# Twelve instead of eight of the 22 up tiles of a gated MLP as transposed seven-product blocks, and both token sublayers in a new order

## The chip, the cores and the metric

The kernel runs on one core of a Trainium2 chip. The metric is the device time of one execution in microseconds (us). TensorE is called PE here, VectorE DVE, ScalarE ACT, GpSimd POOL and SyncE SP; PEld is the loading of weights into PE, which runs beside its matmuls.

## The reference, cut to what matters

Two layers (`DEPTH` = 2) on 512 tokens of width 1024, everything in f32. Each layer has a token sublayer and a channel sublayer:

```python
proj = x @ w_in[i]                       # q, k, v of two kinds of heads, and three gates
ya = neighbourhood_attention(...)        # 8 heads of 64
yb = bidirectional_retention(...)        # 4 heads, chunks of 128 tokens
merged = sigmoid(gate_a) * (ya @ w_branch_a[i]) + sigmoid(gate_b) * (yb @ w_branch_b[i])
x = layer_norm(ALPHA * x + merged @ w_out[i], ...)
h = x @ w_up[i]                          # 1024 -> 2 * 2816, then a convolution of width 3 over tokens
ffn = (gelu(a) * b) @ w_down[i]          # a, b: the two halves of the convolved h
ple = sigmoid(x @ w_ple_gate[i]) * (p[i] @ w_ple_proj[i])
x = layer_norm(ALPHA * x + ffn + ple, ...)
```

## The kernel before, in words

**Arithmetic.** Each f32 matrix is carried as two fp32r matrices, hi and lo (`split`, L177: ACT casts hi, DVE subtracts hi from the source and gives lo). A product is three matmuls, hi·hi, hi·lo and lo·hi (`mm3`, L432; their records have L434, L435 and L436). Where `_Ordered` (L95) holds an engine to the order of the program, everything that is issued through it shows as L109.

**Seven products.** Most of the large matrix products run as 2x2 block products in seven steps instead of eight: a, c, t1, t2, d, t3 and t4, of which t1, t2, d and t3 take sums of blocks of the activations and sums of blocks of the weights. The results go through two PSUM pairs, u and v, and a third one for c.

**Weights.** All weights lie in DRAM in chunks of 128x1024 (512 KB). `Stream` (L304) holds the list of all chunks in the order of their use. It loads a chunk by a DMA that SP issues (`fetch`, L348), adds a second block to it, where a sum is wanted, by an accumulating DMA that POOL issues (`add`, L335; L342), and splits it (`prep`, L373). A few items are "sent": ACT makes hi and then minus hi in the place of lo, and a DMA of POOL adds the weights to that (L392 to L394), so that DVE has nothing to do with them. The `HELD`, `EARLY` and `DEEP` tables say where a raw chunk lies and how far ahead of its use it is loaded and split.

**Token sublayer.** The combined projection runs first as blocks of seven products for v and gates (`VG`), with the heads' q and k, the attention and the retention woven in by the list `FILL`. `bb` (L1153) is the product with `w_branch_b`, `ba` (L1141) that with `w_branch_a`; `turn` (L1131) transposes the merged rows; `proj_ln` (L511) is the output projection with the layer norm, and its transposes are in `done1` (L1292). `plain_x` (L1117) brings the residual in rows: in layer 0 it only loads it, in layer 1 it loads the normalised values and multiplies by the gain and adds the bias on DVE (L1126, L1127), four times each over 128x1024. It is called at product number `XN_AT` of `bb`.

**Channel sublayer.** 22 up tiles are handled in segments of 6, 8 and 8 (`SEGS` counts pairs); each segment's down product (`D0`, `D1`, `D2` below) follows its up tiles. A **plain up tile** (`up_tile`, L1342) is two halves of 8 x 3 = 24 matmuls of 128x512, 48 in all; each half then has a convolution: one ACT pass (L1331) and two DVE passes (L1332, L1333) over 512 tokens. The halves are multiplied, and `take` (L1381) splits the result for the down product's "a" operand (128x256), its "k" operand (128x512) and, per pair of tiles, four sums (`s_parts`, L1366 to L1369) that are split into sa and sb. An **up block** (`up_block`, L1435) computes four up tiles with the roles of weights and activations exchanged, as seven products of 48 matmuls of 128x256, 336 in all. Its results go to six side tiles (`h`) through ACT copies and DVE additions; the convolutions, gelu and products of its four tiles are "chores", queued at product t3 (`lin`) and at t4 (`gates`, `third` is L1481), and taken off the queue in such numbers per matmul group as `CHORES` says.

Before the change segments 1 and 2 have a block each: 8 of the 22 tiles. The order in them is a list, `UB`, of products and plain tiles. Segment 0 has six plain tiles. Five of them are woven into the embedding's gate (`pg`, L1540: seven products of 24 matmuls of 128x512 for x @ w_ple_gate, order `PG`), so that an up tile stands between most of the gate's products, and the sixth follows. Then the down product of segment 0 begins with its product a, which wants the "a" operands of all three pairs; t1 wants sa. `into` (L1686, L1687) adds results to the residual R.

Of the kernel before, what the change touches and what calls it, by code (L numbers as in the profile page):

```python
# [32 lines left out]
SENT = (('k3', 'q2'), ('k2', 'k3', 'nk2', 'nq3', 'q1'))  # L33
HELD = {3: ('a', 'd', 't2', 't3', 't4'), 4: ('a', 'c', 'd', 't2', 't4')}
XT_HELD = (('t3',), ('t3', 't4'))
DEEP = 5

FILL = (('2c', '3t2', '3d', 'nk1', 'vn', '3t3', '3t4', '2t1', 'nk2', '2t2', '2d', '2t3', '0a', 'nq2', 'k2', '0t1', '2t4', '0t2', '0d', '0t3', '1a', 'q0',
# [3 lines left out]
BB = ("a", "c", "t1", "d", "t2", "t3", "t4")  # L42
RET_AT = ((33, 32, 38, 37), (31, 38, 36, 39))
NA_AT = ((10, 13, 13, 16, 18, 19, 20, 23), (6, 9, 9, 10, 11, 11, 17, 20))
# [3 lines left out]
OUT_PREP = ((0, 1, 1, 1), (0, 1, 1, 1))  # L48
# [3 lines left out]
VG = (('p0', 'p1', '3a', 'nq0', 'nk3', 'nq3', '3c', '3t1', 'nk0', '2a', 'nq1'), ('3a', '2a', '2c', '3c', '3t1', 'nq0', 'nk1', 'nk0', '3t2'))  # L52

XN_AT = (6, 6)
M_AT = (1, 5)
TABLES_AT = (0, 6)
REST_AT = (1, 1, 1, 1, 7, 8)
PEND_AT = (1, 3)

PG = ("a", "c", "up", "t1", "up", "t2", "up", "d", "up", "t3", "up", "t4")  # L60
PG_HELD = ("t1", "t2", "t3", "t4")
PG_EARLY = "a"
PG_DEEP = 5
UB = ((), ('up', 'up', 'a', 'c', 'up', 't1', 't2', 'd', 't3', 't4', 'up'), ('a', 'up', 'c', 't1', 'up', 't2', 'd', 't3', 't4', 'up', 'up'))
UB_HELD = (('t1', 't2', 't3', 't4'), ('a', 'd', 't2', 't3', 't4'), ('c', 't2', 't3', 't4'))
UB_EARLY = ('a', 'a', 'c')
UB_DEEP = (5, 4, 5)
MLP_ORD = ORD
FIN_ORD = (None, 't1')
MLP_DEEP = 4  # L70
MLP_LOOK = 4
SEG_ORD = ((1, 0), (0, 0), (0, 0))
CHORES = ((4, 4, 4), (4, 1, 3), (4, 0, 7))
S_LOAD_AT = (0, 0, 3)
RES_DMA = (0, 1)
TR_AT = ("c",)
S_AT = ("up0", "t1", "t2", "up1")
A_DEEP = (4, 4, 3)
BOUND = ("p0", "t4a", "tr", "t4b", "p1")
VG_DEEP = 3  # L80
VG_EARLY = 'd'
VG_HELD = (('0c', '0t2', '1a', '1c', '1t2', '1t4', '2a', '2t4', '3t1', '3t2'),
 ('0a', '0c', '0d', '0t3', '1c', '1t4', '2a', '2c', '2t1', '2t3', '3a', '3c', '3d', '3t1', '3t2', '3t3'))
ON_CHIP = (('', '', 't2', ''), ('', '', '', ''))
BB_HELD = (('t2',), ('c', 'd', 't1', 't2', 't4'))
BB_EARLY = ('a', 'a')
RC_ACT = ((0, 2, 3, 5, 6, 7), (3, 4, 6))
# [38 lines left out]
def trunk(tc, wpack, x_nat, x_tr, head, p_tr, rpb, decay, ln_par, ln_col, conv, cos_t, sin_t, dist, xi_d, zd, ident_d, out):  # L126
# [4 lines left out]
    with ExitStack() as es:  # L131
# [49 lines left out]
        class Item:  # L181
# [7 lines left out]
            def __init__(self, kind, src, width, pool=None, plus=None, own=None):  # L189
                self.kind, self.src, self.width, self.pool, self.plus, self.own = kind, src, width, pool, plus, own  # L190
                self.raw = self.hl = None
                self.nxt = self.early = self.block = self.other = None

                self.sent = False

        def block_items(pos, held, early, onchip=""):
# [3 lines left out]
            for kind, src, plus in (("a", "a", None), ("c", "c", None), ("t1", None, "b"), ("t2", None, "d"),  # L200
                                    ("d", "d", None), ("t3", "b", "d"), ("t4", None, "c")):
                for j in range(2):
# [6 lines left out]
                    if kind == "t3":  # L209
                        [o for o in out if o.kind == early][j].early = it  # L210
                    out.append(it)
            ds = [o for o in out if o.kind == "d"]
            for kind in onchip.split():
                for it, d in zip([o for o in out if o.kind == kind], ds):
                    it.other, d.own = d, True
            return out

        def down_items(l, s):
# [11 lines left out]
            held = {k: up for k in HELD[n]}  # L230
# [1718 lines left out]
```

## Time and profile before

| | |
|---|---|
| median of 3 runs | 1684.34 us (1683.64 to 1687.1) |
| the profiled execution | 1689.1 us, its span 1687.3 us |
| granted clock of PE, mean | 0.997 |
| busy: PE, PEld, DVE | 98%, 83%, 78% of the span |
| busy: ACT, POOL | 59%, 14% |

PE's busy time is modelled and leaves out little; the time of a stage is better read from the distance of its matmuls. In the profiled execution the embedding's gate and the MLP of layer 0 stand at these times (us): the gate with five up tiles 462.7 to 556.5, the sixth up tile to 567.4, D0 to 596, segment 1's up tiles to 680, D1 to 721, segment 2's to 805, then D2. The last matmul begins at 1677.5.

### The profile page before, as it was taken

The numbers are of one execution on the slowest core, as the hardware profiler recorded it, in microseconds if no ns is written. First come the engines' busy times: TensorE is split into PE (matmuls) and PEld (weight loads), VectorE is DVE, ScalarE is ACT, GpSimd is POOL, SyncE is SP. The second block draws the span as 40 slices with busy tenths as digits, with TensorE's granted clock in tenths as the row PEclk, the third lists the DMA queues.
The fourth block names the chain that finished last, engine by engine and source line by source line (L and its number), as shares of the span: only waits on it lengthen the run. The fifth ranks groups of instructions, "written<-read, shape, count | busy, mean of one in ns | idle before, by whom it ended". The sixth has DMA issues, their size and how long they took to land.

```text
span 1687.3 us, 22720 instructions
## 1 busy us (share of the span) xinstructions
PE 1656.4 (98%) x8391; PEld 1399.0 (83%) x8391; DVE 1314.1 (78%) x2019; ACT 996.3 (59%) x1520; POOL 232.2 (14%) x277
## 2 busy tenths in 40 slices
PE   8999999999999999999999999999999999999997
PEld 6788888887888889789888888888877888898986
DVE  5847688979687867959976676788897887588598
ACT  5858876635266636546486888464533664474462
POOL 0102101110111111111111011010202111111112
PEclk9999999999999999999999999999999999999999
DMA  8857846556774788697686669544767767787874
GB/s 298 223 169 200 206 98 171 168 161 175 233 208 157 174 272 211 157 258 198 182 239 191 187 163 237 163 100 126 187 205 231 218 180 205 220 202 186 249 194 81
DMA packets 94719, 324.13 MB, mean 192 GB/s; under 512 B 10896, under 2 KB 11408, under 8 KB 94608
## 3 DMA queue, kind: packets, MB, share of 16 engines
q0 software_dynamic: 33840, 121.13, 36.7%
q1 hardware_dynamic: 60768, 201.55, 33.0%
q8 instruction: 66, 1.08, 0.2%
q14 instruction: 45, 0.37, 0.1%
HBM read 295.37 MB, written 26.21 MB: 191 GB/s over the span
## 4 chain that ended last, share of the span: by engine, by line
PE 59%; DVE 14%; issue 13%; DMA 8%; ACT 3%; POOL 1%; SPq 0%; DVEq 0%; POOLq 0%; ACTq 0%
PE u L435 4%; PE u L436 4%; PE u L434 4%; DMA rawa<-in_wpack 4%; PE gt L434 4%; PE gt L435 4%; PE gt L436 4%; PE gt L109 3%; DVE lo L179 3%; PE gn L436 3%; PE gn L434 3%; PE gn L435 3%; PE v L434 3%; PE v L436 3%; PE v L435 3%
## 5 line engine op out<-in xcount | busy, mean ns | idle before, releaser
L179 DVE TENSOR_TENSOR lo<-raw,hi 128x1024 fp32r<-128x1024 f32 (+1 forms) x156 | 188.9, 1217 | 97.6 <-ACT hi L178 97.0
L178 ACT CAST hi<-raw 128x1024 fp32r<-128x1024 f32 (+1 forms) x156 | 161.6, 1045 | 151.1 <-DMA raw<-in_wpack 57.7
L179 DVE TENSOR_TENSOR lo<-rawa,hi 128x1024 fp32r<-128x1024 f32 (+1 forms) x151 | 180.3, 1201 | 64.0 <-ACT hi L178 63.0
L178 ACT CAST hi<-rawa 128x1024 fp32r<-128x1024 f32 (+1 forms) x151 | 154.4, 1032 | 125.9 <-DMA rawa<-in_wpack 49.7
L342 POOL DMA_DIRECT2D rawa<-in_wpack x111 | 98.2, 885 | 624.9 <-DVE lo L179 481.7
L109 PE MATMUL gt<-x1t,hi 128*128 128x512 f32 x384 | 118.3, 389 | 0.0
L434 PE MATMUL gt<-x1t,hi 128*128 128x512 f32 x256 | 99.7, 390 | 0.0
L435 PE MATMUL gt<-x1t,hi 128*128 128x512 f32 x256 | 99.7, 390 | 0.0
L436 PE MATMUL gt<-x1t,lo 128*128 128x512 f32 x256 | 99.6, 389 | 0.0
L434 PE MATMUL gt<-xt,hi 128*128 128x512 f32 x216 | 84.7, 392 | 1.1 <-DVE t L886 0.7
L109 PEld LDWEIGHTS gt<-x1t,hi 128*128 128x128 f32 x384 | 72.1, 188 | 15.0
L435 PE MATMUL gt<-xt,hi 128*128 128x512 f32 x216 | 84.2, 390 | 0.0
L436 PE MATMUL gt<-xt,lo 128*128 128x512 f32 x216 | 84.2, 390 | 0.0
L342 POOL DMA_DIRECT2D rawt<-in_wpack x38 | 33.8, 890 | 309.7 <-DMA rawt<-in_wpack 116.2
L109 PE MATMUL gt<-x1t,lo 128*128 128x512 f32 x192 | 74.9, 390 | 0.1
L109 DVE TENSOR_TENSOR lo<-raw,hi 128x1024 fp32r<-128x1024 f32 (+1 forms) x46 | 54.5, 1197 | 5.2 <-ACT hi L109 4.9
L436 PEld LDWEIGHTS gt<-x1t,lo 128*128 128x128 f32 x256 | 48.1, 188 | 10.1
L434 PEld LDWEIGHTS gt<-x1t,hi 128*128 128x128 f32 x256 | 48.1, 188 | 9.6
L435 PEld LDWEIGHTS gt<-x1t,hi 128*128 128x128 f32 x256 | 48.1, 188 | 9.5
L179 DVE TENSOR_TENSOR lo<-rawt,hi 128x1024 fp32r<-128x1024 f32 (+1 forms) x36 | 42.8, 1193 | 14.8 <-ACT hi L178 14.6
L436 PE MATMUL gn<-hi,mt 128*128 128x512 f32 x128 | 49.3, 391 | 1.5 <-DVE mt L179 1.5
L435 PE MATMUL u<-lo,s 128*128 128x512 f32 x128 | 50.4, 394 | 0.0
(499 smaller groups left out, 5128.6 us busy)
## 6 DMA issues: line engine op xcount, KB each, us to landing
raw<-in_wpack SPq DMA_DIRECT2D x205, 512.0 KB, 4.8
rawa<-in_wpack POOLq DMA_DIRECT2D x124, 512.0 KB, 7.1
rawa<-in_wpack SPq DMA_DIRECT2D x42, 512.0 KB, 6.2
rawt<-in_wpack SPq DMA_DIRECT2D x42, 512.0 KB, 6.0
rawt<-in_wpack POOLq DMA_DIRECT2D x42, 512.0 KB, 7.6
s<-s_scr POOLq DMA_DIRECT2D x32, 512.0 KB, 11.7
s_scr<-s POOLq DMA_DIRECT2D x16, 512.0 KB, 5.1
r_scr<-pp SPq DMA_DIRECT2D x8, 512.0 KB, 10.6
```

The costliest lines, as they stand in the source:

```text
L109: r = f(*a, **k)
L178: nc.scalar.copy(hi, src)
L179: nc.vector.tensor_sub(lo, src, _f(hi))
L342: nc.gpsimd.dma_start(it.raw[:, :w], wpack[l, c][:, o:o + w], accum_op=ALU.add)
L434: nc.tensor.matmul(ps, lh, rh, start=start, stop=False, skip_group_check=more)
L435: nc.tensor.matmul(ps, lh, rl, start=False, stop=False, skip_group_check=more)
L436: nc.tensor.matmul(ps, ll, rh, start=False, stop=stop, skip_group_check=more)
```

## The change

Names of functions stay; the tables now have one entry for each layer, and the line numbers of the changed kernel are larger (L177 becomes L196, L1332 becomes L1413, L1481 becomes L1562, L1687 becomes L1776, L109 becomes L128).

- **A third block.** `UBP` = 1: the last four tiles of segment 0 are a block too. Its products, "Ua" to "Ut4", and the two plain tiles that stay are woven into the gate's order `PG`. "Ut4", the last, is followed by the down product's a. 12 of the 22 tiles are then in blocks. In numbers: 384 matmuls of 128x512 go, 672 of 128x256 come.
- **Other orders in segments 1 and 2** (`UB`): the last plain tile of segment 1 now stands ahead of the block's last product, which is c instead of t4; in segment 2 one plain tile goes from the end to between d and t3, and c to between t3 and t4. In segment 1 the convolutions of the gate half stand ahead of the addition of product c to their source, which nothing reads afterwards (for both layers, the first 256 tokens of four tiles are without c).
- **Weights.** 46 more items are sent, so that 46 casts on ACT and 46 DMAs on POOL take the place of as many subtractions on DVE. Of the accumulating DMAs for sums of chunks 18 go, and the 2 sums that POOL made on chip; 36 sums are made by DVE on chip instead, from chunks that are loaded anyway. SP issues 4 loads more. No weights are kept in the unit of xt any more.
- **Token sublayers.** New `VG`, `FILL`, `RET_AT`, `NA_AT`, `REST_AT` and others. In layer 1 gain and bias of the residual are put on R's tiles early, between the token sublayer's fillers (`early_x`, at `PX_AT`), and stored then; `plain_x` only loads. In layer 0 ACT scales the retention's result (`GN_ACT`) instead of DVE. The additions of the residual in the gate are all on DVE again (`RES_DMA` empty: 8 DVE instructions for 4 DMAs of POOL). The decay constants are loaded earlier. Instructions on PE: 288 more; on DVE 22 more; on ACT 62 more, with 8 loads of tables less among them; POOL 22, SP 4 more.

The diff, cut:

```diff
-SENT = (('k3', 'q2'), ('k2', 'k3', 'nk2', 'nq3', 'q1'))
+SENT = (('k0', 'nk2', 'nq2', 'q0', 'q2', 'q3'), ('k2', 'nq1', 'q3'))
-VG = (('p0', 'p1', '3a', 'nq0', 'nk3', 'nq3', '3c', '3t1', ...
+VG = (('p0', 'p1', '3a', '3c', 'nk1', 'nq1', '2a', 'nk3', 'nq0', '3t1'), ...
-PG = ("a", "c", "up", "t1", "up", "t2", "up", "d", "up", "t3", "up", "t4")
-UB = ((), ('up', 'up', 'a', 'c', 'up', 't1', 't2', 'd', 't3', 't4', 'up'), ('a', 'up', 'c', 't1', 'up', 't2', 'd', 't3', 't4', 'up', 'up'))
+PX_AT = (4, 15, 16, 17, 18, 18, 38, 40, 41, 42)
+GN_ACT = ((0, 1, 2, 3), ())
+PG = (('a', 'c', 'up', 't1', 'up', 't2', 'Ua', 'Ut1', 'd', 't3', 'Ut2', 'Ud', 'Ut3', 't4', 'Uc', 'Ut4'), ...
+UBP = (1, 1)
+M_SENT = (('D0a', 'D1a', 'D1c', 'D2a', 'D2c', 'U2a', 'U2d', 'u10', 'u11', 'u13', 'u14', 'u16', 'u2'), ...
+UB = (((), ('up', 'up', 'a', 't1', 'up', 't2', 'd', 't3', 't4', 'up', 'c'), ('up', 'a', 't1', 'up', 't2', 'd', 'up', 't3', 'c', 't4', 'up')), ...
-CHORES = ((4, 4, 4), (4, 1, 3), (4, 0, 7))
+CHORES = (((4, 0, 0), (2, 2, 2), (8, 0, 9)), ...
-RES_DMA = (0, 1)
+RES_DMA = ((), ())
...
+                    if it.other is not None:
+                        o = it.other
+                        if o.raw is None:
+                            self.fetch(o)
+                        nc.vector.tensor_add(it.raw[:, :it.width], it.raw[:, :it.width], o.raw[:, :it.width])
...
-                        nc.vector.tensor_scalar_mul(y, y, r[:, i:i + 1])
+                        if h in GN_ACT[l]:
+                            nc.scalar.activation(y, y, AF.Copy, scale=r[:, i:i + 1])
+                        else:
+                            nc.vector.tensor_scalar_mul(y, y, r[:, i:i + 1])
...
-                    if l:
-                        nc.vector.tensor_mul(z, z, g)
-                        nc.vector.tensor_add(z, z, b)
+            def early_x():
+                g, b = ln_consts(l - 1, 1)
+                yield
+                for t in range(5):
+                    if t < 4:
+                        nc.vector.tensor_mul(RX[t], RX[t], g)
+                        yield
+                    if t:
+                        nc.sync.dma_start(scr[(t - 1) * P:t * P, :], RX[t - 1])
+                    if t < 4:
+                        nc.vector.tensor_add(RX[t], RX[t], b)
+                    yield
...
+                ub = up_block(0) if UBP[l] else None
+                    if key[0] == "U":
+                        ub(key[1:])
+                        residual()
+                        continue
```

Three places show what the tables move. The first is PE at the start of the program: the last matmuls of the first product (u, of "3a" in `VG`) and what follows. Before, the q of an attention head followed (gt):

```order
L109 MATMUL u_244<-lo_201,xt_106 128x512
L109 MATMUL u_244<-hi_200,xt_106 128x512 x2
L109 MATMUL u_244<-lo_201,xt_106 128x512
L109 MATMUL u_244<-hi_200,xt_106 128x512
L109 MATMUL gt_324<-xt_106,hi_245 128x512 x2
L109 MATMUL gt_324<-xt_106,lo_246 128x512
```

Now the same block's product c follows (w, "3c"):

```order
L128 MATMUL u_252<-lo_161,xt_106 128x512
L128 MATMUL u_252<-hi_160,xt_106 128x512 x2
L128 MATMUL u_252<-lo_161,xt_106 128x512
L128 MATMUL u_252<-hi_160,xt_106 128x512
L128 MATMUL w_307<-hi_208,xt_106 128x512
L128 MATMUL w_307<-lo_209,xt_106 128x512
```

The q product has moved behind c and the k and q of another head; what follows the first product needs one chunk of the same block instead of a chunk of q.

The second place is DVE at the end of segment 0's up tiles in layer 0, beside the down product's first matmuls. Before, the sixth plain tile's convolution (ca) and its sums (ta, tb) stood there, and the additions to R:

```order
L109 SCALAR_TENSOR_TENSOR ca_5132<-gt_5107,cw_568,ca_5132 128x511 x2
L1687 TENSOR_TENSOR R_4280<-R_4280,u_5141 128x512
L109 TENSOR_TENSOR ca_5099<-ca_5099,ca_5132 128x512
L1687 TENSOR_TENSOR R_4281<-R_4281,u_5142 128x512
L1366 TENSOR_TENSOR ta_5174<-ca_5099,ca_4978 128x256
L109 TENSOR_TENSOR k_936_5138<-ca_5099,k_936_5138 128x512
L1367 SCALAR_TENSOR_TENSOR tb_5175<-ta_5174,ca_4978 128x256
L1368 TENSOR_TENSOR tb_5175<-ca_4978 128x256
L1369 SCALAR_TENSOR_TENSOR ta_5174<-tb_5175,ca_5099 128x256
```

Now the gate halves of the block's four tiles (h) stand there, first their convolutions, then their products (L1562) and the subtractions for the "a" operand, then the k operands and two sets of sums:

```order
L1414 SCALAR_TENSOR_TENSOR hc_5145<-h_4817,cw_660,hc_5145 128x511
L1413 SCALAR_TENSOR_TENSOR h_5311<-h_4753,cw_660,h_5311 128x511 x2
L1414 SCALAR_TENSOR_TENSOR h_5311<-h_4753,cw_660,h_5311 128x511
L1413 SCALAR_TENSOR_TENSOR h_5315<-h_4755,cw_660,h_5315 128x511
...
L1562 SCALAR_TENSOR_TENSOR h_5311<-h_5311,hc_5121 128x512
L1414 SCALAR_TENSOR_TENSOR h_5315<-h_4755,cw_660,h_5315 128x511
L198 TENSOR_TENSOR a_829_4515<-h_5311,a_829_4515 128x256
L1562 SCALAR_TENSOR_TENSOR h_5315<-h_5315,hc_5145 128x512
L1562 SCALAR_TENSOR_TENSOR h_5311<-h_5311,hc_5121 128x512
L198 TENSOR_TENSOR a_950_5341<-h_5315,a_950_5341 128x256
L1562 SCALAR_TENSOR_TENSOR h_5315<-h_5315,hc_5145 128x512
```

In this place DVE's work of one tile has become that of four.

The third place is DVE in layer 1's output projection, between the last rows of merged values (sa) and their transposed splits (mt). Before:

```order
L1179 TENSOR_TENSOR sa_10672<-sa_10672,M_11308 128x512
L1126 TENSOR_TENSOR xn_11366<-xn_11366,lng_11362 128x1024
L1127 TENSOR_TENSOR xn_11366<-xn_11366,lnb_11363 128x1024
L1126 TENSOR_TENSOR xn_11370<-xn_11370,lng_11362 128x1024
L1126 TENSOR_TENSOR xn_11374<-xn_11374,lng_11362 128x1024
L1127 TENSOR_TENSOR xn_11370<-xn_11370,lnb_11363 128x1024
L1127 TENSOR_TENSOR xn_11374<-xn_11374,lnb_11363 128x1024
L1126 TENSOR_TENSOR xn_11378<-xn_11378,lng_11362 128x1024
L179 TENSOR_TENSOR mt_11422<-tr_11416,mt_11421 128x4x128
```

After the change:

```order
L1253 TENSOR_TENSOR sa_10821<-sa_10821,M_11474 128x512
L198 TENSOR_TENSOR mt_11638<-tr_11632,mt_11637 128x4x128
L198 TENSOR_TENSOR mt_11638<-tr_11641,mt_11637 128x4x128
L198 TENSOR_TENSOR mt_11654<-tr_11648,mt_11653 128x4x128
L198 TENSOR_TENSOR mt_11654<-tr_11657,mt_11653 128x4x128
L198 TENSOR_TENSOR lo_11674<-raw_11548,hi_11673 128x1024
```

The eight passes of gain and bias over 128x1024 have left this place; they stand among the fillers now.

More of the change, by code (lines that the diff above doesn't have):

```diff
@@ L258, in ub_items @@
                     out += [Item("w", (l, UP0 + 2 * n + i, 0, 1024), 1024) for i in range(2)]
+                    for it in out[-2:]:
+                        it.sent = f"u{n}" in M_SENT[l]
                     n += 1
@@ L722, in step @@
                         product(kind, st["u"], True)
+                        while hooks:
+                            next(hooks.pop(0))
                         st["p1"] = copies(st["u"], "p1")
@@ L1253, in fillers @@
                 for i, f in enumerate(F):
+                    for g in steps.get(len(keys) + i, ()):
+                        next(g, None)
                     if f == "vn":
@@ L1870, in _pack @@
     su = _stat(w_up)
-    blocks = [2 * sum(SEGS[:s + 1]) - 4 for s in range(3) if UB[s]]
+    blocks = [2 * sum(SEGS[:s + 1]) - 4 for s in range(3) if UB[l][s] or (UBP[l] and s == 0)]
     for i in range(NF):
```

239 lines of the change are left out of this document (147 added, 92 removed), and 6 rows, old and new, of the table FILL.

## The prediction

> **What bounds the kernel now.** I read the page's first lines, then the DMA queues, then the windows around every stage that has waits, then PE's waits in those windows, then DVE's groups of instructions.
>
> ```profile
> span 1687.3 us, 22720 instructions
> PE 1656.4 (98%) x8391; PEld 1399.0 (83%) x8391; DVE 1314.1 (78%) x2019; ACT 996.3 (59%) x1520; POOL 232.2 (14%) x277
> q0 software_dynamic: 33840, 121.13, 36.7%
> q1 hardware_dynamic: 60768, 201.55, 33.0%
> ```
>
> PE is the bound: 31 us of the span are without a matmul. The sum below is made against the profiled execution, 1689.1 us with a span of 1687.3; it lies 4.8 above the median of 1684.34, and I apply the difference that I find to the median. The queues give a price for transfers: 121.13 MB are 231 loads of 512 KB (0.524 MB) in 36.7% of 1687.3, so 2.68 us of all 16 engines for one issued by POOL, and the same way 1.45 us for one issued by SP.
>
> The windows view gives for each stretch the busy time and count of PE, PEld, DVE, ACT and POOL, then the granted clock, the DMA share and GB/s. Five products of an up block lie in the first row, two plain up tiles in the second; the next two are the end of segment 1's up tiles in each layer, then the end of segment 0's, and the gate with its up tiles; then the up tiles of segments 1 and 2.
>
> ```profile
> 640.20:668.90 28.70, 28.70 (x241) 28.70 (x240) 21.62 (x25) 18.44 (x23) 4.90 (x6) 1.00 0.94 240
> 782.90:804.70 21.80, 21.80 (x99) 18.04 (x98) 21.50 (x30) 16.59 (x26) 2.58 (x3) 1.00 0.76 165
> 680.00:704.00 24.00, 23.20 (x97) 17.19 (x95) 24.00 (x41) 14.86 (x22) 3.46 (x4) 1.00 0.55 114
> 1514.00:1540.00 26.00, 25.07 (x106) 18.86 (x105) 26.00 (x44) 15.58 (x22) 3.46 (x4) 1.00 0.59 118
> 567.00:596.00 29.00, 29.00 (x130) 24.02 (x129) 24.86 (x35) 15.00 (x19) 4.88 (x7) 1.00 0.78 225
> 463.00:556.50 93.50, 93.45 (x416) 77.16 (x415) 77.51 (x105) 62.47 (x86) 13.66 (x18) 1.00 0.65 183
> 596.00:680.00 84.00, 84.00 (x530) 76.47 (x529) 57.74 (x73) 45.77 (x60) 13.33 (x18) 1.00 0.82 223
> 721.00:805.00 84.00, 84.00 (x530) 76.39 (x529) 62.20 (x80) 48.33 (x65) 12.08 (x17) 1.00 0.82 224
> ```
>
> In the MLP PE waits almost nowhere but at the end of segment 1, where DVE is busy for the whole window. The token sublayers lose more:
>
> ```profile
> 0.00:76.00 76.00, 69.42 (x289) 53.34 (x289) 50.88 (x84) 48.66 (x76) 6.94 (x13) 1.00 0.84 257
> 380.00:417.00 37.00, 32.95 (x151) 26.30 (x150) 34.85 (x50) 19.94 (x30) 1.83 (x3) 0.95 0.59 160
> 1205.00:1285.00 80.00, 73.88 (x341) 59.30 (x340) 72.74 (x95) 33.84 (x49) 8.56 (x9) 1.00 0.74 218
> ```
>
> **The change part by part.**
>
> *Matmuls.* The first window has 240 matmuls of 128x256 in 28.7 us, 119.6 ns each; PEld is busy in all of it, so weight loading sets the pace. The second has 96 of 128x512 in 21.8 us, 227 ns each. A block of four tiles takes 336 x 0.1196 = 40.2 us, four plain tiles 192 x 0.227 = 43.6. One more block a layer: 2 x -3.4 = **-6.8 us**. This term is firm as long as PE is fed. By the Trainium skill, "TensorE: Matmul & The Clock Gate", section "Back-to-back issue gap", the isolated gap is N/2.4 + 2.5 ns, which as an estimate is 109 and 216 ns and would make this -9.5; the rows are wider by 5 to 10%, most at the small size, and the same section says that loading weights costs spacing there, which fits the full PEld.
>
> *End of segment 0.* DVE's prices are in its groups (line, operation, shapes, count, then busy and mean ns of one):
>
> ```profile
> L179 DVE TENSOR_TENSOR lo<-raw,hi 128x1024 fp32r<-128x1024 f32 x154 | 187.7, 1224 | 97.6 <-ACT hi L178 97.0
> L1687 DVE TENSOR_TENSOR R<-R,u 128x512 f32<-128x512 f32 x42 | 27.0, 680 | 0.0
> L1332 DVE SCALAR_TENSOR_TENSOR h<-h,cw,h 128x511 f32<-128x511 f32 x16 | 11.8, 745 | 2.8 <-ACT h L1331 2.7
> L1481 DVE SCALAR_TENSOR_TENSOR h<-h,hc 128x512 f32<-128x512 f32 x16 | 10.8, 683 | 0.0
> L179 DVE TENSOR_TENSOR a<-h,a 128x256 fp32r<-128x256 f32 x8 | 3.3, 416 | 0.0
> L1366 DVE TENSOR_TENSOR ta<-h 128x256 f32<-128x256 f32 x8 | 3.3, 418 | 0.0
> L179 DVE TENSOR_TENSOR sa<-ta,sa 128x512 fp32r<-128x512 f32 x18 | 12.4, 687 | 2.7 <-ACT sa L178 2.7
> ```
>
> The block's last product, Ut4, gives what the gate halves' convolutions need, and D0's product a follows at once. From there to the last sb that product t2 reads, the changed order has on DVE 9 convolution passes (6.7 us), 4 products (2.7), 2 subtractions for a (0.8), 2 for k and 4 for sa and sb (4.1), 8 passes for ta and tb (3.3), 2 additions to R (1.4), and a lo of 128x512 and one of 128x1024 (1.9): 33 instructions, 21.0 us. Instructions that follow one another overlap a little:
>
> ```profile
> 1249.38 2.35 DVE L1126 TENSOR_TENSOR xn<-xn,lng 128x1024 f32<-128x1024 f32 x2
> 1251.65 2.35 DVE L1127 TENSOR_TENSOR xn<-xn,lnb 128x1024 f32<-128x1024 f32 x2
> ```
>
> Two passes of 1.22 us take 2.27 from start to start, 0.085 less for each, so the 33 take 18.2 us at best. PE has a product of 18 matmuls each for a, c and t1, and 12 of t2, ahead of that sb: 66 x 0.227 = 15.0 us. The wait is 18.2 - 15.0 = 3.2 us to 21.0 - 15.0 = 6.0, wherever along a to t2 it falls. Reckoned in the same way by starts, DVE's surplus at the end of segment 1 before is 2.2 us, and the windows above lose 2.0 (24.0 - 97 x 0.227) and 1.9 (26.0 - 106 x 0.227); so I take 4.0, nearer to the lower end: **+8** for two layers (6.4 to 12.0). Before there was one tile of such work there, and no wait. What queues behind DVE meanwhile is the lo of the next weights; these have the same 15 us of cover.
>
> *End of segment 1.* The last plain tile now has the block's product c behind it, 48 x 0.1196 = 5.7 us of matmuls that nothing waits for, ahead of D1. That covers the loss of 2.0 and 1.9 us: **-3** (-3.9 to 0; not all, since the block's gates come closer to D1).
>
> *Start.* PE's waits in the first window (waiting line, what it waited for, us, times, longest):
>
> ```profile
> PE gt L109 <- DVE lo L109: 2.2, 1, 2.2
> PE gt L109 <- ACT xt L109: 1.2, 1, 1.2
> PE v L109 <- ACT s L109: 1.0, 1, 1.0
> PE w L435 <- DVE lo L109: 0.7, 1, 0.7
> PE gt L109 <- DVE xt L109: 0.2, 1, 0.2
> ```
>
> Those of q products (gt) on a weight's lo and on the transposed x are what the new order moves away, since product c follows instead; it wants two chunks as well. The five make 5.3 us; bounds -5.3 and, if c's chunks are later than q's, +2.2 (the same wait again). I take about half, **-2.5**.
>
> *Layer 0, before the output projection, and layer 1's output projection.* First the waits from 380 to 417 us, then four of those from 1205 to 1285:
>
> ```profile
> PE u L435 <- DVE lo L179: 2.0, 1, 2.0
> PE tr L1134 <- DVE sa L1179: 1.6, 1, 1.6
> ...
> PE tr L1298 <- DVE xn L509: 1.7, 1, 1.7
> PE gn L436 <- DVE mt L179: 1.5, 1, 1.5
> PE u L434 <- ACT mt L178: 1.2, 1, 1.2
> ...
> PE tr L1134 <- DVE sa L1179: 0.5, 1, 0.5
> ```
>
> In layer 0 the pool of sums and gates on DVE gets lighter by the 16 scalings that go to ACT and by one sent chunk; ACT is busy 19.94 of 37 us there and has room. Of 3.6 us of waits and 1.8 of a slow clock (below) I take **-2** (-5.4 to +1.6, the second wait again). In layer 1 eight passes of 1.22 us (two of the rows above, from 1246.98 to 1257) leave DVE just ahead of mt: 9.1 us by starts. Two waits on DVE follow, one on ACT that is fed by it, and one on xn. They make 4.9; I take half, **-2.5** (-4.9 to 0). The passes are hidden among the fillers, where DVE's share is below PE's; without that cover they would cost the 9.1.
>
> *Weights.* Per layer POOL's and SP's loads, counted in the changed order, are in the gate stage 24.5 and 17, 24.5 x 2.68 + 17 x 1.45 = 90.3 us of 16 engines in 89.5 us of matmuls (before 15 and 22, 72.1); in segment 2 24 and 16, 87.5 us in 83.9 (before 17 and 16, 68.8). D1 ahead of segment 2 has 30.4 us of transfers in 38.1. DVE gains 46 x 1.22 us by the sent chunks and loses about as much to 36 sums on chip, so I count that as nothing. If loads run ahead, these cost nothing; a share above 1 in a stage that follows a slack one costs little: **+1** (0 to 20, below).
>
> Sum: -6.8 + 8 - 3 - 2.5 - 2 - 2.5 + 1 = **-7.8 us**: 1681.3 for an execution like the profiled one, and 1684.34 - 7.8 = **1676.5** for the median.
>
> **The rivals.**
>
> *The new wait is longer and slows the clock.* Three stretches in layer 0:
>
> ```profile
> 385.00:387.80 2.80, 0.81 (x6) 0.38 (x3) 2.80 (x4) 2.80 (x5) 0.00 (x0) 1.00 0.60 190
> 387.80:391.40 3.60, 3.59 (x9) 2.83 (x10) 3.60 (x6) 1.39 (x4) 1.73 (x2) 0.53 0.86 187
> 391.40:395.00 3.60, 3.60 (x18) 2.95 (x17) 3.44 (x5) 0.55 (x1) 0.00 (x0) 1.00 0.96 174
> ```
>
> After 2.0 us of waiting the granted clock was 0.53 for 3.6 us, which held 9 matmuls instead of 16: about 1.8 us more. With 6.0 of wait and this, a boundary costs 7.8, both 15.6. With -7.0 from the token sublayers the sum is -0.2: 1684. Against it: the waits of seg 1's end did not slow the clock (1.00 in both rows). The same page of the Trainium skill, "What's actually happening", puts the half rate behind an idle window of about 3.4 us; by that only one wait of over 3.4 us would do it, while here 2.0 us were enough once, and the trace decides.
>
> *The order of the token sublayers gains nothing.* The waits only change their names: -6.8 + 8 - 3 + 1 = -0.8, so 1683.5. For it: each of these places has DVE at 67 to 94% of the window; against it: nine us of DVE do leave the last one.
>
> *Slower: transfers become the bound in the gate stage and in segment 2.* The highest share that a long stretch shows is 0.94 (640.2 to 668.9). If the engines carry no more, the gate stage takes 90.3/0.94 = 96.1 instead of 89.5, and D1 with segment 2 takes 117.9/0.94 = 125.4 instead of 122.0: 10.0 us per layer, 20 in all, so -8.8 + 20 = +11.2, **1695.5**. It turns to slower by 0.2% where less than about 0.955 is carried (5.0 + 1.4 us per layer). For it: a chunk that is sent goes over the engines twice, and its accumulation has to land before the lo can be used; 0.82 stands for whole segments before. Against it: the stage ahead of the gate has room to load ahead, and 0.96 is shown in the last row above.
>
> *All better.* The boundary's wait falls under cover and the token waits go whole: -6.8 + 2 - 3.9 - 5.3 - 3.6 = -17.6, 1666.7. That the change does not do what it says can be left out, since the order shows the block's matmuls.
>
> **How the numbers follow.** The forecast has 0.52, the long wait 0.13, no gain in the token sublayers 0.11, the transfers 0.16, all better 0.08. Of the forecast's own range (bounds of its terms added as independent, about 1668 to 1685) a small part lies in the same bin. About 0.2% (3.4 us) is what a measurement of this kernel can tell from no change. Faster: 0.46 + 0.08 + 0.06 from the two middle cases = 0.60. Same: 0.05 + 0.13 = 0.18; slower: 0.16, and 0.06 from middle cases that miss by more = 0.22. The range goes from 1666, all better, to 1696, the transfers; it leaves out about 0.1 on each side.
>
> **What would show it.** Right: in the profile after, 128x256 matmuls still 120 ns apart, PE's waits in D0 on DVE's a, k, sa or sb of 3 to 6 us per layer with DVE busy throughout, none at the start of D1, and no wait of a tr on xn of over 1 us in layer 1. Wrong: PE waits on lo by a DMA of POOL in the gate stage or segment 2, with the DMA share over 0.94 (the slower rival); no wait in D0 (then the cover is larger than I counted); waits of the same size at the start and in both output projections.

## The result and the profile after

| | before | after |
|---|---|---|
| median, us | 1684.72 (1683.55 to 1687.17, 6 runs) | 1677.86 (1672.91 to 1681.56, 6 runs) |
| ratio, 95% interval | | 0.9958 (0.9945 to 0.9971) |
| profiled execution, its span | 1689.1, 1687.3 | 1681.56, 1679.8 |

The change gains 6.9 us by the medians (4.9 to 9.3 by the interval), 7.8 were forecast. The forecast is right in sign and size. Its terms are not: two large errors of opposite sign cancel.

The page of the changed kernel answers to the first lines shown of before:

```profile
span 1679.8 us, 23451 instructions
PE 1647.5 (98%) x8679; PEld 1409.4 (84%) x8679; DVE 1327.7 (79%) x2041; ACT 1044.8 (62%) x1582; POOL 247.3 (15%) x299
q0 software_dynamic: 37296, 133.19, 39.8%
q1 hardware_dynamic: 61344, 203.65, 33.8%
```

PE's busy time is 8.9 us less, transfers by POOL take 39.8% of the span instead of 36.7%. The windows view of the stages that the prediction spoke of (busy time and count of PE, PEld, DVE, ACT, POOL, then granted clock, DMA share, GB/s): the start; the output end of the token sublayer in layer 0 and in layer 1; the end of segment 0 in both layers; the end of segment 1 in both; the gate stage; segment 2 in layer 0.

```profile
0.00:76.00 76.00, 74.02 (x316) 58.35 (x317) 55.43 (x90) 53.07 (x82) 9.69 (x16) 1.00 0.94 286
360.00:412.00 52.00, 50.00 (x234) 39.82 (x233) 48.09 (x67) 35.87 (x49) 6.95 (x8) 1.00 0.66 172
1195.00:1275.00 80.00, 76.85 (x359) 62.89 (x358) 65.11 (x88) 38.20 (x54) 10.47 (x11) 1.00 0.79 231
552.40:589.20 36.80, 32.07 (x128) 24.21 (x128) 30.81 (x49) 20.96 (x30) 7.74 (x12) 0.95 0.62 173
1384.40:1422.80 38.40, 32.03 (x129) 24.49 (x128) 31.45 (x50) 22.62 (x32) 7.75 (x12) 0.96 0.61 170
660.00:690.00 30.00, 30.00 (x156) 25.82 (x155) 27.71 (x48) 20.96 (x32) 5.21 (x6) 1.00 0.95 229
1494.00:1524.00 30.00, 30.00 (x156) 25.82 (x155) 27.71 (x49) 20.96 (x32) 5.21 (x6) 1.00 0.92 222
461.00:552.40 91.40, 91.40 (x563) 82.58 (x562) 78.40 (x101) 59.92 (x79) 20.32 (x26) 1.00 0.90 227
711.00:795.00 84.00, 82.49 (x522) 74.85 (x521) 54.23 (x71) 55.27 (x71) 15.64 (x18) 1.00 0.97 248
```

The start now loses 2 us instead of 6.6. The end of segment 0, where nothing was lost before, now holds D0's 126 matmuls (28.6 us at 227 ns) in 36.8 and 38.4 us, at a mean clock of 0.95 and 0.96. The end of segment 1 loses nothing. Segment 2 loses 1.5 us at a DMA share of 0.97.

For a balance I add up by stage how much later than 227, 120 or 109 ns (128x512, 128x256, 128x128) a matmul starts behind the one ahead of it, where that is over 0.1 us. "Again" is a second profile of the changed kernel (after_again below):

| lost time of PE, us | before | after | again |
|---|---|---|---|
| start, to 100 us | 7.5 | 1.9 | 0.7 |
| layer 0, middle of the token sublayer | 2.8 | 1.3 | 1.5 |
| layer 0, its output end | 6.7 | 3.4 | 3.4 |
| end of segment 0, layer 0 and 1 | 0 + 0 | 8.0 + 9.5 | 8.4 + 4.7 |
| end of segment 1, layer 0 and 1 | 2.5 + 2.1 | 0 + 0 | 0 + 0 |
| layer 1, middle of the token sublayer | 3.1 | 0.9 | 0.9 |
| layer 1, its output end | 8.2 | 4.2 | 4.3 |
| rest (segment 2, gates, the last segment) | 1.0 | 3.5 | 2.9 |
| sum | 33.8 | 32.8 | 26.8 |
| span less this sum | 1653.5 | 1647.0 | 1647.5 |

The last row is PE's own work: 6.5 and 6.0 us less, where -6.8 was worked out. The token sublayers give 16.6 us back in the first profile, and the ends of segment 0 take 17.5. The three profiled executions lie at the edges of their kernels' times: that of before (1689.1) is above the six in the table, that of the changed kernel is the slowest of its six, "again" the fastest of its five. So the balance says where time is lost, and the medians say how much the change gives.

### The profile page after: what moved, and what is told of

Same layout as the page of the kernel before. It is cut to its first block, busy times and chain, and to the rows that moved or that the text cites. A ratio compares the mean times of both kernels' runs of the same rounds, so it can differ in the third digit from the quotient of the medians.

```text
span 1679.8 us, 23451 instructions
## 1 busy us (share of the span) xinstructions
PE 1647.5 (98%) x8679; PEld 1409.4 (84%) x8679; DVE 1327.7 (79%) x2041; ACT 1044.8 (62%) x1582; POOL 247.3 (15%) x299
## 3 DMA queue, kind: packets, MB, share of 16 engines
q0 software_dynamic: 37296, 133.19, 39.8%
q1 hardware_dynamic: 61344, 203.65, 33.8%
## 4 chain that ended last, share of the span: by engine, by line
PE 84%; DVE 6%; DMA 5%; ACT 2%; issue 2%; POOL 0%; DVEq 0%; SPq 0%; POOLq 0%; ACTq 0%
PE u L493 6%; PE u L495 6%; PE u L494 6%; PE gt L495 6%; PE gt L493 6%; PE gt L494 6%; PE v L493 4%; PE u L128 4%; PE v L494 4%; PE v L495 4%; PE gn L493 4%; PE gn L494 4%; PE gn L495 4%; PE gt L128 4%; PE v L128 3%
## 5 line engine op out<-in xcount | busy, mean ns | idle before, releaser
L197 ACT CAST hi<-raw 128x1024 fp32r<-128x1024 f32 (+1 forms) x114 | 118.0, 1044 | 89.0 <-DMA raw<-in_wpack 37.9
L198 DVE TENSOR_TENSOR lo<-raw,hi 128x1024 fp32r<-128x1024 f32 (+1 forms) x114 | 136.7, 1210 | 45.4 <-ACT hi L197 44.6
L495 PE MATMUL gt<-x1t,lo 128*128 128x512 f32 x256 | 99.8, 390 | 2.2 <-DMA lo<-in_wpack 2.2
L493 PE MATMUL gt<-x1t,hi 128*128 128x512 f32 x256 | 99.8, 390 | 0.0
L494 PE MATMUL gt<-x1t,hi 128*128 128x512 f32 x256 | 99.7, 390 | 0.0
L451 POOL DMA_DIRECT2D lo<-in_wpack x49 | 42.5, 867 | 350.4 <-ACT lo L450 336.0
L128 DVE TENSOR_TENSOR lo<-rawa,hi 128x1024 fp32r<-128x1024 f32 x39 | 46.9, 1221 | 13.6 <-ACT hi L128 13.6
L493 PEld LDWEIGHTS gt<-x1t,hi 128*128 128x128 f32 x256 | 48.1, 188 | 9.6
L494 PEld LDWEIGHTS gt<-x1t,hi 128*128 128x128 f32 x256 | 48.1, 188 | 9.5
L128 ACT CAST hi<-rawa 128x1024 fp32r<-128x1024 f32 (+1 forms) x43 | 43.3, 1026 | 19.3 <-DMA rawa<-in_wpack 9.6
L450 ACT ACTIVATE lo<-hi 128x1024 fp32r<-128x1024 f32 x49 | 51.9, 1058 | 0.9
L197 ACT CAST hi<-rawt 128x1024 fp32r<-128x1024 f32 (+1 forms) x38 | 39.0, 1029 | 21.4 <-PE u L494 5.5
L493 PE MATMUL u<-hi,s 128*128 128x512 f32 x128 | 50.1, 392 | 0.0
## 6 DMA issues: line engine op xcount, KB each, us to landing
s<-s_scr POOLq DMA_DIRECT2D x32, 512.0 KB, 10.6
```

Source lines behind the costliest of these rows:

```text
L128: r = f(*a, **k)
L197: nc.scalar.copy(hi, src)
L198: nc.vector.tensor_sub(lo, src, _f(hi))
L450: nc.scalar.activation(lo[:, :w], _f(hi[:, :w]), AF.Copy, scale=-1.0)
L451: nc.gpsimd.dma_start(lo[:, :w], wpack[l, c][:, o:o + w], accum_op=ALU.add)
L493: nc.tensor.matmul(ps, lh, rh, start=start, stop=False, skip_group_check=more)
```

## The experiments

Each time is a median, each ratio is to the kernel before on the same chip with its 95% interval. Theory A, formed from the balance above: the token orders carry the gain, and the third block costs more at the end of segment 0 than its matmuls save. Rival B: the terms as predicted.

| run | us | ratio |
|---|---|---|
| block_alone | 1690.82 | 1.0029 (1.0016 to 1.0041) |
| tokens_alone | 1670.18 | 0.9908 (0.9887 to 0.9930) |
| t4_behind | 1685.36 | 1.0003 (0.9991 to 1.0014) |
| t4_behind_chores | 1698.62 | 1.0079 (1.0064 to 1.0095) |
| seg1_upup | 1706.60 | 1.0121 (1.0098 to 1.0145) |
| seg1_upup_chores | 1691.38 | 1.0024 (1.0012 to 1.0035) |
| unsent_u14_u16 | 1674.44 | 0.9931 (0.9918 to 0.9943) |
| late_x | 1682.66 | 0.9984 (0.9975 to 0.9993) |
| after_again | 1678.38 | 0.9954 (0.9942 to 0.9966) |
| eight_blocks | 1674.48 | 0.9934 (0.9922 to 0.9946) |
| eight_unsent | 1673.98 | 0.9932 (0.9919 to 0.9944) |
| tokens0_before | 1684.66 | 0.9989 (0.9980 to 0.9999) |

**The two halves: block_alone and tokens_alone.** In the first the tables of the token sublayers are those of before, and plain_x is as before; in the second those of the gate and the MLP:

```diff
 # block_alone
-VG = (('p0', 'p1', '3a', '3c', 'nk1', ...
+VG = (('p0', 'p1', '3a', 'nq0', 'nk3', ...
 # tokens_alone
-UBP = (1, 1)
+UBP = (0, 0)
-PG = (('a', 'c', 'up', 't1', 'up', 't2', 'Ua', 'Ut1', ...
+PG = (("a", "c", "up", "t1", "up", "t2", "up", "d", ...
```

> The changed kernel with the token sublayers' tables and the residual's gain and bias as before; the MLP and the gate are those of the changed kernel. Theory A (the profile after is right on the stages: the third block saves 6.8 us of matmuls and 4.6 at segment 1's end, and costs 17.5 at segment 0's end and 3 in segment 2; the token orders gave the rest): -6.8 - 4.6 + 17.5 + 3 = +9, 1694 us. Rival B (the terms as predicted hold for most executions, and the profiled one is an unlucky one): -6.8 + 8 - 3 + 1 = -0.8, 1684 us.

> The changed kernel with the gate and the MLP of before (eight of the 22 tiles in blocks, no weights of the MLP sent); the token sublayers are the changed ones. Theory A: the start gives 5.6 us, the middle of both token sublayers 1.5 and 2.2, the two output ends 3.3 and 4.0, -16.6 in all: 1668 us. Rival B: -7, 1678 us.

The block with its MLP alone is 4.9 us slower than before (1.0029; 2.7 to 6.9), the token orders alone are 15.5 us faster (0.9908). Theory A's 9 and -16.6 are nearer than rival B's -0.8 and -7, and only theory A has the sign of both, though its 9 is nearly twice the 4.9. The sum of the two, -10.6, is more than the whole change gives (-6.9 and -7.8 in its two measurements), but the intervals, the token orders' of 11.8 to 19.0 above all, leave open whether this difference is real. In the profile of block_alone the waits on a at the end of segment 0 are 2.0 us each and the clock stays up; it loses 5.2 and 5.3 us there, 10.5 in place of 17.5 and 13.1.

**A product for cover: t4_behind and t4_behind_chores.** The gate's last product is moved behind the block's last one:

```diff
-PG = (( ... 'd', 't3', 'Ut2', 'Ud', 'Ut3', 't4', 'Uc', 'Ut4'), ...
+PG = (( ... 'd', 't3', 'Ut2', 'Ud', 'Ut3', 'Uc', 'Ut4', 't4'), ...
 # t4_behind_chores besides
-PG_CHORE = (1, 1)
+PG_CHORE = (8, 8)
```

> The changed kernel with one entry of the gate's order moved: the gate's product t4 (24 matmuls, 5.5 us) now stands behind the block's last product Ut4, ahead of the down product. Theory A (PE waits at the end of segment 0 for the chain from Ut4 to the first operand a of the block's tiles: copy, convolution, gelu with its table, product, cast; the slow clock follows from that wait): the 5.5 us cover the waits of 2.9 and 4.7, the clock stays up (1.7 each), and some of the small waits behind go: -10, 1668 us. Rival C (the amount of DVE's work is what counts, so the wait only moves to the next operands): not more than 3 us better, 1675 us or above.

It was slower by 7.5 us, so theory A's 10 us fall. The wait became longer. PE's wait at D0 in layer 0 of t4_behind, and then the point on ACT where the gelus begin, 7.5 us behind t4's last matmul (551.6):

```profile
PE u L492 <- ACT a L196: 7.0, 1, 7.0
```

```profile
559.09 1.28 ACT L1558 ACT_TABLE_LOAD   x1 [3.98 <-DVE h L1413]
```

The chores are issued per chunk of a gate product, one each; moved to the end, t4 pops two of the four linear convolutions, and the gates are issued only by D0, behind the gate's own sigmoids and additions to R. The row above says what ACT waited for, 3.98 us: DVE, which has no gap from 547.4 us until the first a is there, with eight passes of the linear convolutions and four for R ahead of the gate halves. This suggests that cover helps only if the chain is in the engines' queues before the cover's own work. The next kernel tests that:

> As t4_behind (the gate's product t4 behind the block's Ut4), but eight chores instead of one are issued with each chunk of a gate product, so that the convolutions, gelus and products of the block's tiles stand on ACT and DVE ahead of t4's own results instead of behind them. Theory A, mended (PE waits for the chain behind Ut4, and cover counts only if the chain's instructions are queued ahead of the covering product's own): the waits of 8.1 and 7.1 us on a go to under 1.5 each with no slow clock, 14 us better than t4_behind and 8 to 10 better than the changed kernel, 1668 to 1671 us. Rival C (the amount of DVE's work counts): the wait stays above 5 us a layer, 1680 or more.

PE's waits at D0 in layer 0 of t4_behind_chores, and ACT there:

```profile
PE v L492 <- ACT hi L127: 4.7, 1, 4.7
PE v L492 <- ACT sa L196: 3.5, 1, 3.5
PE u L492 <- ACT a L127: 0.6, 1, 0.6
```

```profile
555.21 1.28 ACT L127 ACT_TABLE_LOAD   x1 [3.90 <-DVE h L127]
556.51 0.63 ACT L127 ACTIVATE h<-h 128x512 f32<-128x512 f32 x1
557.04 0.80 ACT L127 ACTIVATE h<-h,cw 128x512 f32<-128x512 f32 x1
557.75 1.03 ACT L127 CAST hi<-rawa 128x1024 fp32r<-128x1024 f32 x1
```

The wait on a is 0.6 us, as theory A had it, but the time is 13 us worse again: the cast of the next weights (hi) now stands in ACT's queue behind the gelu's table, which waited 3.90 us for DVE, and the sums (sa) come later too. Rival C's forecast (waits above 5 us, 1680 or more) came in, theory A is right only about which wait came first. That the amount of work alone makes the waits is not shown by this: the wait on hi comes from the order on ACT, since that cast needs nothing of the block's chain.

**Segment 1: seg1_upup and seg1_upup_chores.** Two plain tiles behind t4 in place of one tile and product c, so that c takes part in the gate half again:

```diff
-UB = (((), ('up', 'up', 'a', 't1', 'up', 't2', 'd', 't3', 't4', 'up', 'c'), ...
+UB = (((), ('up', 'a', 't1', 'up', 't2', 'd', 't3', 'c', 't4', 'up', 'up'), ...
 # seg1_upup_chores besides
-CHORES = (((4, 0, 0), (2, 2, 2), (8, 0, 9)), ...
+CHORES = (((4, 0, 0), (4, 2, 2), (8, 0, 9)), ...
```

> The changed kernel with another order in segment 1: up, a, t1, up, t2, d, t3, c, t4, up, up, so that two plain tiles stand behind the block and its product c takes part in the gate half again. Theory A (what took away the wait ahead of D1 is cover behind the block's last product; two tiles, 21.8 us of matmuls, cover as well as a tile and product c): no wait at D1, within 1.5 us of the changed kernel's 1677.9. Rival D (it was that product c, last, has no reader, so that DVE had less to finish ahead of D1): the waits of 2.5 and 2.1 us come back, 1682.5 us.

> As seg1_upup, but four chores instead of two are taken with each half of a plain tile in segment 1, so that 16 instead of 8 are issued behind t4 ahead of D1. Theory A, mended: the waits on k and a at D1 (9.0 and 5.3 us in both layers) and the slow clock behind them go, about -17; the wait of product t1 on its weights' hi and lo in segment 1 (6.1 and 1.2 us) stays, since the chunks' places are those of another order: 1688 us. Rival D (two tiles in place of tile and product c do not cover): above 1700 us.

PE's waits in segment 1 and at D1 of layer 0, first seg1_upup, then seg1_upup_chores:

```profile
PE w L492 <- ACT k L196: 4.5, 1, 4.5
PE v L492 <- ACT hi L196: 2.6, 1, 2.6
```

```profile
PE v L492 <- ACT hi L196: 2.5, 1, 2.5
PE w L492 <- ACT k L196: 1.8, 1, 1.8
```

With 16 instead of 8 chores issued ahead of D1 the wait on k goes from 4.5 to 1.8 us and the kernel gains 15 of the 29 us that seg1_upup had lost. But this k is that of the last plain tile, which now stands right ahead of D1, and in seg1_upup DVE stood idle ahead of this tile's last convolution. It waited for weights for a sum on chip that was queued there (6.65 us in layer 1):

```profile
683.32 1.23 DVE L429 TENSOR_TENSOR rawt<-rawt,rawd 128x1024 f32<-128x1024 f32 x1 [6.55 <-DMA rawd<-in_wpack]
```

In seg1_upup_chores DVE has no such gap. So more than the number of chores differs, and that their tempo is a part of the cover is not shown. The block's own operands were in time in seg1_upup: product a of D1 ran without a wait. (The 5.3 us on a that the second expectation puts at D1 are the waits at the end of segment 0, 2.5 and 2.8.) The wait on hi, that of product t1 on its weights, stays; the places of the weights are still those of the other order. Neither theory's time came in (1677.9 and 1682.5; 1706.6 was measured). Whether another order keeps c and the cover at no cost stays open.

**Sent chunks: unsent_u14_u16.**

```diff
-M_SENT = (('D0a', 'D1a', 'D1c', 'D2a', 'D2c', 'U2a', 'U2d', 'u10', 'u11', 'u13', 'u14', 'u16', 'u2'), ...
+M_SENT = (('D0a', 'D1a', 'D1c', 'D2a', 'D2c', 'U2a', 'U2d', 'u10', 'u11', 'u13', 'u2'), ...
```

> The changed kernel with the up tiles 14 and 16 split by ACT and DVE instead of sent, so that 4 lo's a layer come from DVE. Theory A (PE's waits of 1.5 and 0.6 us in segment 2 are the POOL DMA that has to land in lo): these waits go, DVE has 1.2 us more per chunk where it isn't behind: 1.5 to 2 us better, 1676 us. Rival F (the engines of the DMA are the bound there, as the DMA share of 0.9 says, and not this one step): the wait moves to other chunks, 1678 us.

It is 3.9 us better than after_again (0.9931 against 0.9954, with intervals that touch), at least as much as theory A had. There is no wait on POOL's DMA left in segment 2, and none has moved to other chunks, which rival F expected. But four transfers a layer have left the engines too: the DMA share from 705 to 795 us is 0.93 where after_again has 0.97. So the run does not tell one late step from engines that are too full. About 2 of the 3.9 us are lost time of segment 2 in the two profiles.

**The residual's gain and bias: late_x.** `plain_x`, `early_x` and the stores are those of before:

```diff
+                    if l:
+                        nc.vector.tensor_mul(z, z, gx)
+                        nc.vector.tensor_add(z, z, bx)
...
-                px = early_x()
-                for i in PX_AT:
-                    at_key(i, px)
```

> The changed kernel with the residual's gain and bias in layer 1 where they were before (eight DVE passes over 128x1024 in bb, at the load). Theory A (these 9.1 us of DVE were what PE waited for at the end of layer 1's token sublayer): the waits on mt and xn return, 3 to 4 us, 1681.5 us. Rival G (the new order of the fillers made the room, the passes themselves are hidden): not over 1 us, 1678.5 us.

It is 4.3 us worse than after_again. PE's waits from 1195 to 1290 us in late_x, and then in the changed kernel:

```profile
PE gn L495 <- DVE mt L198: 2.3, 1, 2.3
PE tr L1213 <- DVE sa L1258: 1.7, 1, 1.7
PE gn L494 <- DMA lo<-in_wpack: 1.6, 1, 1.6
PE v L493 <- ACT yw L862: 1.5, 1, 1.5
```

```profile
PE tr L1208 <- DVE sa L1253: 1.6, 1, 1.6
PE v L493 <- ACT yw L862: 1.4, 1, 1.4
```

The wait on mt is back, with one on a sent chunk's lo: this stage loses 8.9 us in place of 4.2. Theory A holds in size and for mt, though the wait on xn did not return; rival G falls.

**Layer 0's token order: tokens0_before.** The entries of layer 0 in all tables of the token sublayer are those of before.

```diff
-VG = (('p0', 'p1', '3a', '3c', 'nk1', ...
+VG = (('p0', 'p1', '3a', 'nq0', 'nk3', ...
-GN_ACT = ((0, 1, 2, 3), ())
+GN_ACT = ((), ())
```

> The changed kernel with layer 0's token sublayer in the order of before; layer 1's is the changed one. Theory A (the stages of the two profiles: start 5.6, middle 1.5, output end 3.3 us): 10.4 worse than the changed kernel, 1688 us. Rival B (the predicted terms for layer 0, 2.5 and 2): 1682.4 us.

It is 6.3 us worse than after_again, between the two. Its profile loses 5.8 us at the start, 2.5 in the middle and 6.7 at the output end (0.7, 1.5 and 3.4 in after_again), 9.4 more in all, near what theory A said; the median has two thirds of that. The profiled execution of tokens0_before is the slowest of its 12 and that of after_again the fastest of its five, which may be the difference. PE's waits from 0 to 76 us with layer 0's old order:

```profile
PE gt L124 <- ACT xt L124: 1.4, 1, 1.4
PE warm L596 <- DVE warm L593: 1.2, 1, 1.2
PE w L490 <- DVE lo L124: 0.7, 1, 0.7
PE gt L124 <- DVE xt L124: 0.2, 1, 0.2
```

With the new order only the warm-up's wait and one of 0.8 us on a lo are left in that window.

**The third block by itself: eight_blocks, eight_unsent, after_again.**

```diff
 # eight_blocks
-UBP = (1, 1)
+UBP = (0, 0)
-PG = (('a', 'c', 'up', 't1', 'up', 't2', 'Ua', 'Ut1', ...
+PG = (("a", "c", "up", "t1", "up", "t2", "up", "d", ...
 # eight_unsent besides
-M_SENT = (('D0a', 'D1a', ...
+M_SENT = ((), ())
```

> The changed kernel once more, on the chip of the three runs beside it, so that small differences are taken there: 1678 us, within 1.5. Theory A (a wait of 2.5 to 4.7 us at the end of segment 0 slows the clock in some executions and not in others, as the profiles so far have 2.7 to 9.5 us for that end): its executions spread by 5 us or more, with the mean clock lower in the slower ones; a rival without this, under 3 us like the kernel before.

> The changed kernel without its third block: the gate with five plain tiles between its products and a sixth behind, as before; segments 1 and 2, what is sent, and the token sublayers stay as changed. Theory A (the end of segment 0 costs 9.3 to 17.5 us in the profiles with the third block, 12.5 in the middle, and the block's matmuls save 6.8): 5.7 better than the changed kernel, 1672 us. Rival B (8 for the ends as predicted, so a net cost of 1.2): 1676.7 us. Rival H (the third block pays): above 1679 us.

> As eight_blocks, and no weights of the MLP are sent (18 splits a layer go back to DVE, and 18 transfers of POOL go). Theory A (sent chunks make the waits of segment 2, and DVE has room for their splits but at the ends of the segments): the waits on POOL's DMA go, 1 to 3 better than eight_blocks, 1670 us, about as the kernel with the MLP of before. Rival J (sending is what keeps DVE ahead at the ends): 2 us worse than eight_blocks, 1674 us.

Without the third block the kernel is 3.9 us faster than after_again (1674.48 against 1678.38; ratios 0.9934 and 0.9954, whose intervals overlap a little), between theory A's 5.7 and rival B's 1.2, and the runs do not choose between these; rival H is out. The window in which D0's start cost 8 us has PE almost without a gap in eight_blocks:

```profile
552.40:589.20 36.80, 36.61 (x161) 29.67 (x160) 27.78 (x39) 16.99 (x22) 9.50 (x14) 1.00 0.88 243
```

With no weights of the MLP sent, eight blocks have 0.9932, and twelve with two tiles unsent have 0.9931. Once the waits on sent chunks are gone, the third block is worth nothing that the runs can tell: its profile has 7.6 us more of lost time (24.5 against 16.9) and 7.7 us less of PE's own work (1646.3 against 1654.0). Sending by itself made no difference to eight blocks that the runs can tell; the intervals are too wide to exclude theory A's -2 or rival J's +2.

The executions of after_again spread by 4.1 us, those of the kernel before on that chip by 5.7, so theory A's claim on the spread is not borne out there; in the table of the result it was 8.7 against 3.6, so it stays open.

The lowest ratio of all is that of tokens_alone: the new token sublayers with the gate and the MLP of before, 0.9908, with all of product c in the gate half. It was measured on another chip than the eight-block kernels, and the intervals overlap.

## Why the prediction came out right, step by step

- *Matmuls, -6.8.* Right: PE's own work went from 1653.5 to 1647.0 and 1647.5. The 9.5 worked out from the Trainium skill's gap ("TensorE: Matmul & The Clock Gate", section "Back-to-back issue gap") would have been too much; the rows of before gave the better price.
- *End of segment 0, +8.* The step that failed. I let PE run on 66 ready matmuls and compared them with DVE's work up to the last sb of t2. But only the matmuls of the first pair, six each of a, c and t1, have their operands when Ut4 ends: 18 matmuls, 4.1 us. Then PE stands at the first a of the block's tiles. ACT at the end of segment 0 in layer 1 (start, duration, operation, and in brackets the idle time ahead and what ended it):

```profile
1384.61 1.05 ACT L128 CAST hi<-rawa 128x1024 fp32r<-128x1024 f32 x1 [5.48 <-PE u L128]
1385.56 0.58 ACT L128 COPY h<-u 128x512 f32<-128x512 f32 x1
1386.18 1.52 ACT L1412 ACTIVATE h<-h,cw 128x512 f32<-128x512 f32 x2
1387.61 0.56 ACT L128 COPY h<-u 128x512 f32<-128x512 f32 x1
1388.20 1.52 ACT L1412 ACTIVATE h<-h,cw 128x512 f32<-128x512 f32 x2
1389.74 1.28 ACT L1559 ACT_TABLE_LOAD   x1
1391.03 1.67 ACT L1559 ACTIVATE h<-h 128x512 f32<-128x512 f32 x3
1392.85 0.41 ACT L197 CAST a<-h 128x256 fp32r<-128x256 f32 x1
```

DVE in the same place, just ahead of that cast:

```profile
1391.47 0.74 DVE L1413 SCALAR_TENSOR_TENSOR h<-h,cw,h 128x511 f32<-128x511 f32 x1
1392.13 0.68 DVE L1562 SCALAR_TENSOR_TENSOR h<-h,hc 128x512 f32<-128x512 f32 x1
```

ACT has no gap from the first copy to the cast of a, 7.7 us: two copies, four convolutions, the load of the table and three gelus stand in line ahead of one operand. DVE has none there either, with a weight's lo and eight convolution passes ahead of the product (L1562). The third gelu ends at 1392.70, the product at 1392.81, and the cast begins at 1392.85. The two queues end together, and the prediction had only DVE's.

The first row on ACT is a weight's cast that held up the copy. The view puts its wait down to PE, but in after_again the same cast began 2.7 us ahead of Ut4's end. What it waited for is its chunk, from an accumulating transfer that POOL issued at 1374.04 and that landed 10.5 us later, at 1384.5, just ahead of the cast. The issue, the times to landing of the two such transfers there, and the same cast in layer 0, where the view names the transfer:

```profile
1374.04 1.00 POOL L128 DMA_DIRECT2D rawa<-in_wpack  x1
DMA to landing us min/median/max: 10.4/10.4/10.5
550.70 1.05 ACT L128 CAST hi<-rawa 128x1024 fp32r<-128x1024 f32 x1 [3.59 <-DMA rawa<-in_wpack]
```

In after_again, layer 1, the transfer took 8.2 us. The cast was done ahead of the copy, which could start while Ut4's second half still ran:

```profile
1380.08 1.05 ACT L128 CAST hi<-rawa 128x1024 fp32r<-128x1024 f32 x1 [2.49 <-DMA rawa<-in_wpack]
1381.59 0.59 ACT L128 COPY h<-u 128x512 f32<-128x512 f32 x1 [0.46 <-PE u L128]
```

There the wait was 2.0 us, here it was 4.7. Eight profiles have this end as it is here, in two layers each. In all 16 the cast begins 0.1 us behind the landing of its chunk. In five the cast is done in time, the copy starts 1.2 us ahead of Ut4's end and PE waits 2.0 us; in the other eleven the wait is 3.5 us plus the time from Ut4's end to the copy (negative where the copy is ahead), 2.5 to 4.7. So the queues of ACT and DVE make 2.0 us of the wait, and a late transfer the rest. PE's waits on a in the two layers of the changed kernel's profile:

```profile
PE u L493 <- ACT a L197: 7.4, 2, 4.7
```

Behind them come waits of 0.2 to 0.8 us on weights and on sa, and the clock. So the end of segment 0 cost 17.5 and 13.1 us in the two profiles of the changed kernel and 10.5 to 15.0 in the other six, in all but one above the 12.0 that I had as its upper end, and near the 15.6 of the rival "the new wait is longer and slows the clock". That rival's mechanism is what happened, with the wait at the first a, behind two queues and a transfer, instead of behind DVE's work up to the last sb; its time is off because it had the token sublayers at -7.
- *End of segment 1, -3.* A little more in size: 2.5 and 2.1 us of lost time went whole. That the matmuls of c are the cover fits the trace, but c can stand there only because nothing reads it afterwards, and no run takes the two apart.
- *Start, -2.5; layer 0's output end, -2; layer 1's, -2.5.* All three in the right direction, all too small: -5.6, -3.3 and -4.0. I took half of the waits where nearly all could go. The middles of both token sublayers, which I had at nothing, gave 1.5 and 2.2 more. Together -16.6 in the profiles, and -15.5 in tokens_alone, where I had -7.0. The rival "gains nothing" is out.
- *Weights, +1.* Waits on sent chunks' lo cost 1.5 and 0.6 us in segment 2 in the profile; taking four of the sent chunks a layer away gained 3.9 us. The slower rival is refuted: the gate stage ran without a gap at a DMA share of 0.90, and segment 2 lost 1.5 us at 0.97, above the 0.955 from which I had it slower. That one chunk's chain of casts and transfer is late, and not the engines of the DMA, fits this but is not shown.

So the sum fits by luck. In the profiles 9.5 us too little cost at the end of segment 0 met 9.6 too little gain in the token sublayers; by the medians of the two halves it is 5.7 too little cost (4.9 in block_alone, where -0.8 was worked out) and 8.5 too little gain. The two halves add up to 3 us more than the whole change gives, which their intervals leave open.

## What to carry to other kernels

When a stage is made cheaper on the bounding engine but delivers its results all at once, count the matmuls that are really ready at that point, operand by operand, and put beside them the whole queue of the engine that makes the first missing operand, with its table loads, the casts of weights that stand in it and the transfers that these wait for. More cover did not help in the two runs here: in one the chain stood behind the cover's own work, in the other what the next stage needs stood behind the chain. And a change that moves several things is worth taking apart early: here the new orders of the token sublayers carried all of the gain, and the block gave nothing that the runs could tell.

## What the runs showed of the hardware

A wait of PE of a few us slowed the granted clock in some places and not in others of the same length. The windows of the wait and of what follows, at the end of segment 0 in layer 0, first the changed kernel, then unsent_u14_u16:

```profile
556.50:559.40 2.90, 0.12 (x2) 0.01 (x1) 2.90 (x5) 2.69 (x5) 0.00 (x0) 1.00 0.49 95
559.40:564.50 5.10, 5.10 (x15) 3.87 (x16) 3.87 (x8) 3.23 (x6) 0.00 (x0) 0.67 0.00 0
```

```profile
555.40:558.80 3.40, 0.27 (x3) 0.02 (x1) 3.40 (x6) 3.18 (x5) 0.00 (x0) 1.00 0.54 105
558.80:562.60 3.80, 3.80 (x16) 2.82 (x16) 3.62 (x8) 3.17 (x6) 0.00 (x0) 1.00 0.00 0
```

After a wait of 2.8 us 15 matmuls took 5.1 us at a clock of 0.67; after one of 3.1 us 16 took 3.8 at 1.00. Of the sixteen such waits in eight profiles, 2.0 to 4.7 us long, nine had some eight matmuls at half pace behind them (twice 2.0, 2.5, twice 2.8, 2.9, 3.1, 3.7 and 4.7 us), seven had not (2.0 to 3.1). The Trainium skill, "TensorE: Matmul & The Clock Gate", section "What's actually happening", says that the activity window runs freely and gives this as the reason why the point of change varies; that waits of one length fall differently here agrees with that. With its idle window of about 3.4 us the trace does not agree, since 2.0 us were enough here.
